# The second layer's modulation as VectorE multiply-adds in the first layer's channel mixing

## The chip, the cores and the metric

One core of a Trainium2 chip. TensorE (PE) multiplies matrices into PSUM, VectorE (DVE) and GpSimd (POOL) work elementwise, ScalarE (ACT) applies functions, SyncE (SP) issues the DMAs. The metric is the device time of one execution in microseconds (us); less is better.

## The reference

A trunk of two layers works on 512 latent tokens and 256 context tokens of 1024 channels, in float32. Each layer scales and shifts its normalized input by a modulation that is worked out from two condition vectors, mixes tokens (convolution and attention), and then mixes channels with a squared-ReLU network of 4096 hidden channels:

```python
mx = (silu_c @ w_ada[i] + b_ada[i])[:, None, :]      # latent: 6 x 1024 values
mc = silu_cc @ w_ada[i] + b_ada[i]                    # context
...
x = x + gx2 * sqrelu_mlp(modulate(rmsnorm(x, norm2_g[i]), sx2, ax2), w_mlp1[i], w_mlp2[i])
if not last:
    h_ctx = h_ctx + gc2 * sqrelu_mlp(modulate(rmsnorm(h_ctx, norm2_g[i]), sc2, ac2),
                                     w_mlp1[i], w_mlp2[i])

def sqrelu_mlp(h, w1, w2):
    return jnp.square(jax.nn.relu(h @ w1)) @ w2
```

The context stream is not needed behind the first layer's end, so the second (`last`) layer's channel mixing has the latent tokens alone.

## The kernel before

**Split products.** Every float32 product is made of three: each operand is split into a rounded high half (`Copy` on ScalarE, L76) and a low half (source minus high half, L77, on VectorE or on the engine in `lo_eng`), and `fm_block` issues high x high, high x low and low x high (L104, L105, L106) for 8 blocks of 128 rows: 24 matmuls for 128 output channels and one group of tokens. A group is the 512 latent tokens (`LAT`, a wide block), the 256 context tokens (`CTXS`, narrow), or around a norm the latent half of 256.

**Weight slabs.** `load_slab` loads 1024 x 256 weights (1 MB) into a raw tile by a DMA on SP's queue and splits them in two halves of four row blocks, `h_w` on ScalarE and `l_w` on `lo_eng`; `both` gives the first half to VectorE and the second to GpSimd. There are two raw tiles (tag `raw`) in this stage, which the modulation's slabs share, and two tiles each for the high and the low halves.

**Channel mixing.** It goes over four chunks of 1024 hidden channels (`cch`). In each, four slabs of `w_mlp1` (tiles `f`; ScalarE relu L1146 into `fr` and square L1147 into the high half `fh`, GpSimd square L1148 of `fr` in place, VectorE subtraction L1149 into the low half `fl`), then four slabs of `w_mlp2` (tiles `r`; VectorE adds the gated product to the residual `X`, L1079). A slab is two blocks of output channels for each group. PSUM tiles: two of tag `mm` for latent blocks, two of tag `mc` for context blocks, four of tag `mi` for the small things. The first chunk starts behind the norm `norm2`, in token groups of 256 and with two slabs held at once; in the last chunk of the first layer `out_slabs` does its last two slabs group by group, with `norm1` of the next layer behind each group (row sums, `dg_n` L253, a matmul that broadcasts them, `nb_n`, then the scaled tokens `nu_n`, split into `h1h` and `h1l`).

**Modulation.** The 6144 modulation columns of a layer are 24 slabs of `w_ada`. `ada_slab` loads one, multiplies it on TensorE by `cvec`, the two condition vectors in 32 columns, into four column strips of the array at once (8 matmuls, L216, two records each), copies the result to SBUF (`adasb`, ScalarE, L222), transposes it (two transposes, L225), adds the four strips up (two reductions, L228) and the bias (L231). The first layer's slabs run before and in its token mixing; the second layer's 24 stand in the first layer's channel mixing, in the loops that the diff shows: one after each slab of weights, two after the first group.

**The order of the work.** The program is written as one order of all engines' work. A scheduler puts it into a fixed queue for each engine before the launch, lets later work go ahead where it is ready by its own plan, and gives out the tiles; on the chip each engine takes its queue in order and waits on semaphores.

Of the kernel before, what the change touches and what calls it, by code (L numbers as in the profile page):

```python
# [8 lines left out]
F32 = mybir.dt.float32  # L9
F32R = mybir.dt.float32r  # L10
AF = mybir.ActivationFunctionType
ALU = mybir.AluOpType
AX = mybir.AxisListType

P = 128
D = 1024
KT = D // P
# [22 lines left out]
R_BADA, R_N1, R_N2, R_BG, R_BDW, R_LNG, R_LNB, R_ANG, R_C, R_CC, R_END = (  # L40
    0, 48, 56, 64, 80, 84, 88, 92, 93, 101, 109)
# [10 lines left out]
def trunk_kernel(  # L52
# [6 lines left out]
    nc = tc.nc  # L59
# [19 lines left out]
    def raw_slab(src, name):  # L79
        r = state["tp"].tile([P, KT, 256], F32, tag="raw", name=name, bufs=state["nraw"])  # L80
        nc.sync.dma_start(r, src)
        return r
# [16 lines left out]
    def rows(src, col0, ncols):  # L99
        return src[:, col0 : col0 + ncols].rearrange("(k p) n -> p k n", p=P)  # L100
# [25 lines left out]
    ident = cst[:, C_ID : C_ID + P]  # L126
# [9 lines left out]
    state = {}  # L136
    both = nc.vector, nc.gpsimd
# [71 lines left out]
    def ada_slab(i, L, s):  # L209

        mi = state["mi"]
        r = raw_slab(rows(w_ada[i], 256 * s, 256), f"ada{i}_{s}")
        ps = mi(f"adaps{i}_{s}")
        for k in range(KT):
            j = k % 4
            nc.tensor.matmul(ps[32 * j : 32 * j + 32, :256], cvec[:, k, :], r[:, k, :],  # L216
                             start=k < 4, stop=k >= 4, tile_position=(0, 32 * j))
        if state["nt"] == 3:
            sb = state["tp"].tile([P, 512], F32, tag="t2k", bufs=3, name=f"adasb{i}_{s}")[:, :256]
        else:  # L220
            sb = spool.tile([P, 512], F32, tag="dg", name=f"adasb{i}_{s}", bufs=1)[:, :256]
        nc.scalar.activation(out=sb, in_=ps[:, :256], func=AF.Copy)  # L222
        pc = ps[:, 256:512]
        for m in range(2):
            nc.tensor.transpose(pc[:, m * P : m * P + P], sb[:, m * P : m * P + P], ident)  # L225
        ad = L["ad"][:, :, 2 * s : 2 * s + 2]
        for q in range(2):
            nc.vector.tensor_reduce(  # L228
                out=ad[:, q], in_=pc.rearrange("p (m j r) -> p m j r", m=2, j=4)[:, :, :, q],
                axis=AX.X, op=ALU.add)  # L230
        nc.vector.tensor_tensor(  # L231
            out=ad, in0=ad,
            in1=L["cols"][:, R_BADA + 2 * s : R_BADA + 2 * s + 2].unsqueeze(1)
            .to_broadcast([P, 2, 2]),
            op=ALU.add)

    def ada_gain(L, which, ks=slice(0, KT)):
        par, r0, nm = ((1, R_N1, "A1"), (4, R_N2, "A2"))[which]
# [71 lines left out]
    for t in range(NTT):  # L310
# [4 lines left out]
        if t == 1:  # L315
            L = layer_params(0)
# [17 lines left out]
    for t in range(NTT):  # L334
        xn = xns[t]
        nc.scalar.activation(out=xn, in_=xrs[t], func=AF.Square, accum_out=rs[:, t : t + 1])
        r = rs[:, t : t + 1]
# [5 lines left out]
    cvec = cpool.tile([P, KT, 32], F32, name="cvec")  # L343
# [3 lines left out]
    for s in range(2):  # L347
        nc.vector.tensor_tensor(
            out=cvec[:, :, s], in0=L["cols"][:, R_C + 8 * s : R_C + 8 * s + 8],
            in1=sg[:, 8 * s : 8 * s + 8], op=ALU.mult)  # L350
# [36 lines left out]
    for i in range(DEPTH):  # L387
        last = i == DEPTH - 1
# [4 lines left out]
        cols = L["cols"]  # L393
# [533 lines left out]
        for half, lst in ((1, ga), (0, gc)):  # L927
            for s in range(4):
# [6 lines left out]
                for m in range(2):  # L935
# [3 lines left out]
                    for g in groups:  # L939
                        W = g.stop - g.start  # L940
# [182 lines left out]

        def mlp1_slab(cch, s):
            w1[cch, s] = load_slab(rows(w_mlp1[i], 1024 * cch + 256 * s, 256),
                                   f"w1_{i}_{cch}_{s}", lo_eng=nc.gpsimd if not last and cch + s < 2 else None)

        out_slabs(lambda s: load_slab(rows(w_out[i], 256 * s, 256), f"wo{i}_{s}"),
                  lambda k: (mh[k], ml[k]), gate1, f"o{i}", norm2, None,
# [9 lines left out]
        for cch in range(4):  # L1139
            fh, fl = [None] * KT, [None] * KT  # L1140
            def hidden(w, mb, m, g):
                W = g.stop - g.start
                ps = ps_for(g, f"f{i}_{cch}_{mb}_{g.start}")
                fm_block(ps[:, :W], w, m * P, lambda k: (h2h[:, k], h2l[:, k]), g)
                r = gp.tile([P, 512], F32, tag="ar", bufs=3, name=f"fr{i}_{cch}_{mb}_{g.start}")
                nc.scalar.activation(out=r[:, :W], in_=ps[:, :W], func=AF.Relu)  # L1146
                nc.scalar.activation(out=fh[mb][:, g], in_=r[:, :W], func=AF.Square)  # L1147
                nc.gpsimd.tensor_tensor(out=r[:, :W], in0=r[:, :W], in1=r[:, :W], op=ALU.mult)  # L1148
                nc.vector.tensor_tensor(out=fl[mb][:, g], in0=r[:, :W], in1=f32(fh[mb][:, g]),  # L1149
                                        op=ALU.subtract)  # L1150

# [3 lines left out]
            for s0 in ((0, 2), (2, 3), (3, 4)) if cch == 0 else ((n, n + 1) for n in range(4)):  # L1155
                for s in range(*s0):
                    if (cch, s) not in w1:
                        mlp1_slab(cch, s)
                ws = {s: w1.pop((cch, s)) for s in range(*s0)}
                for g in halves if cch == 0 and s0[0] == 0 else groups:  # L1160
                    for s in range(*s0):
                        for m in range(2):
                            hidden(ws[s], 2 * s + m, m, g)
                if not last and ada_todo:
                    for _ in range(*s0):
                        ada_slab(i + 1, Ln, ada_todo.pop(0))
            fin = cch == 3
            if fin and not last:
                ada_gain(Ln, 0)
# [17 lines left out]

            def after(s):
                if not last and ada_todo:
                    ada_slab(i + 1, Ln, ada_todo.pop(0))  # L1190
                if fin and not last:
                    nc.sync.dma_start(xs_d[i + 1][:, 2 * s : 2 * s + 2, :],
                                      X[:, 2 * s : 2 * s + 2, :])
                if fin and last:
                    for t in range(4):
                        ps = state["mi"](f"oT{s}_{t}")
                        for m in range(2):
                            nc.tensor.transpose(ps[:, m * P : m * P + P],
                                                X[:, 2 * s + m, t * P : t * P + P], ident)
                        ot = gp.tile([P, 512], F32, tag="t2k", bufs=4, name=f"ot{s}_{t}")  # L1200
                        if t % 2:
                            nc.scalar.activation(out=ot[:, :256], in_=ps[:, :256], func=AF.Copy)
                        else:
                            nc.vector.tensor_copy(ot[:, :256], ps[:, :256])
                        nc.sync.dma_start(out[0, t * P : t * P + P, 256 * s : 256 * s + 256],
                                          ot[:, :256])
# [1 line left out]
            out_slabs(  # L1208
                lambda s: load_slab(
                    w_mlp2[i][1024 * cch : 1024 * cch + 1024, 256 * s : 256 * s + 256]  # L1210
                    .rearrange("(k p) n -> p k n", p=P), f"w2_{i}_{cch}_{s}", lo_eng=None if last else both),
                lambda k: (fh[k], fl[k]), gate2, f"r{i}_{cch}",
                norm1 if fin and not last else None, after,
                (lambda: first.update(w=qk_slab(i + 1, 0, nc.gpsimd)),
                 lambda: first.update(v=v_slab(i + 1, 0, nc.gpsimd))) if fin and not last else ())
        if not last:
            while ada_todo:
                ada_slab(i + 1, Ln, ada_todo.pop(0))
            state["ada_done"] = True
            ada_gain(Ln, 1)  # L1220
            L = Ln
# [77 lines left out]
```

## Time and profile before

| | |
|---|---|
| Median of 3 runs | 2418.24 us (2413.56 to 2418.76) |
| The profiled execution | 2414.77 us, of which the span of its instructions is 2413.0 us |
| TensorE clock granted, mean over the span | 0.985 |
| Busy: TensorE matmuls, VectorE, ScalarE, GpSimd | 2322.9, 1381.9, 933.1, 625.2 us |
| First layer's channel mixing | from 842.8 us to about 1440 us of the span |
| Second layer's channel mixing | from 2046.7 us to the end |

The profile is one execution; times in its views are microseconds from the span's start. A row of a timeline has start, duration, engine, line, operation, the tile written and the tiles read, shapes, and a count where equal instructions are merged; in brackets stand the engine's idle time before it and who ended it. A row of a tile's or line's view has count, then shortest, median and longest duration in nanoseconds. A row of groups has, behind the bar, busy time in us and mean duration in ns, then the idle time before with its releasers. The durations of matmuls are modelled and overlap: the distance from start to start tells their cost. "PEld" is the loading of weights, which runs beside the matmuls.

### The profile page before, as it was taken

Reading aid. Unit: us, or ns where it says so; the run is one execution under the profiler, and the core shown is the slowest. Engines: PE = TensorE matmul, PEld = TensorE weight load, DVE = VectorE, ACT = ScalarE, POOL = GpSimd, SP = SyncE. Lnnn points to the kernel's source line nnn. Section 1 sums busy time; section 2 is a strip of 40 time slices with the busy share of each in tenths; the row PEclk is TensorE's granted clock in tenths of the full one; section 3 lists DMA queues with packets and bytes.
Section 4 is the critical chain, followed back from the end, with each engine's and each line's share of the span. In section 5 each row is a group of like instructions: output and inputs, shape, how many; then the busy total and the mean of one; then the engine's idle time right before and its main releaser. Section 6 shows DMA issues by size and latency. Waiting matters only on the chain.

```text
span 2413.0 us, 36865 instructions
## 1 busy us (share of the span) xinstructions
PE 2322.9 (96%) x15034; PEld 2063.4 (86%) x15034; DVE 1381.9 (57%) x2399; ACT 933.1 (39%) x1839; POOL 625.2 (26%) x786
## 2 busy tenths in 40 slices
PE   7999999999999999999999998999999989999999
PEld 6899998878888988888888998989877869888887
DVE  6877877499766452222222357777749966433333
ACT  5555665522333342221312245555542333422331
POOL 2754655010000131120211255655520000200100
PEclk9999999999999999999999999999999999999999
DMA  8111101144445133333333221111114323232322
GB/s 296 53 38 45 45 27 61 42 135 128 157 148 171 45 103 122 110 119 122 106 122 103 68 75 55 43 40 43 42 59 138 127 70 123 88 105 87 105 87 70
DMA packets 222186, 224.79 MB, mean 93 GB/s; under 512 B 5872, under 2 KB 212160, under 8 KB 221888
## 3 DMA queue, kind: packets, MB, share of 16 engines
q1 hardware_dynamic: 222016, 222.43, 28.6%
q8 instruction: 118, 1.93, 0.3%
q14 instruction: 52, 0.43, 0.1%
HBM read 208.73 MB, written 13.67 MB: 92 GB/s over the span
## 4 chain that ended last, share of the span: by engine, by line
PE 83%; DVE 8%; ACT 3%; POOL 2%; issue 2%; DMA 1%; SPq 0%; ACTq 0%; POOLq 0%; DVEq 0%
PE r L104 6%; PE r L106 6%; PE r L105 6%; PE f L104 6%; PE f L105 6%; PE f L106 6%; PE gt L104 3%; PE gt L106 3%; PE gt L105 3%; PE qk L104 2%; PE qk L105 2%; PE qk L106 2%; PE adaps L216 2%; PE yc L113 2%; PE v L104 2%
## 5 line engine op out<-in xcount | busy, mean ns | idle before, releaser
L104 PE MATMUL r<-fh,h_w 128*128 128x512 f32 (+1 forms) x832 | 285.4, 344 | 0.5 <-DVE X L1079 0.5
L104 PE MATMUL f<-h2h,h_w 128*128 128x512 f32 (+1 forms) x832 | 283.6, 344 | 1.3 <-ACT h2h L76 1.0
L105 PE MATMUL f<-h2l,h_w 128*128 128x512 f32 (+1 forms) x832 | 283.5, 342 | 1.1 <-POOL h2l L77 1.0
L105 PE MATMUL r<-fl,h_w 128*128 128x512 f32 (+1 forms) x832 | 283.2, 341 | 0.0
L106 PE MATMUL r<-fh,l_w 128*128 128x512 f32 (+1 forms) x832 | 283.1, 341 | 0.0
L106 PE MATMUL f<-h2h,l_w 128*128 128x512 f32 (+1 forms) x832 | 281.6, 340 | 0.0
L76 ACT ACTIVATE h_w<-r_w 128x1024 fp32r<-128x1024 f32 x128 | 128.7, 1052 | 313.4 <-PE r L105 131.1
L1148 POOL TENSOR_TENSOR fr<-fr 128x512 f32<-128x512 f32 (+1 forms) x104 | 93.2, 898 | 508.8 <-ACT fh L1147 508.8
L894 DVE SCALAR_TENSOR_TENSOR cacc<-z,cols,cacc 128x783 f32<-128x783 f32 (+1 forms) x240 | 203.3, 900 | 0.4
L104 PE MATMUL qk<-h_wqk,h1h 128*128 128x256 f32 x640 | 185.0, 291 | 4.8 <-ACT h1h L76 3.6
L1079 DVE SCALAR_TENSOR_TENSOR X<-r,ad,X 128x512 f32<-128x512 f32 (+1 forms) x104 | 64.9, 627 | 208.4 <-PE r L106 208.2
L105 PE MATMUL qk<-l_wqk,h1h 128*128 128x256 f32 x640 | 182.2, 286 | 0.0
L106 PE MATMUL qk<-h_wqk,h1l 128*128 128x256 f32 x640 | 178.3, 286 | 0.0
L104 PEld LDWEIGHTS f<-h2h,h_w 128*128 128x128 f32 x832 | 156.6, 189 | 25.1 <-ACT fh L1147 2.5
L104 PEld LDWEIGHTS r<-fh,h_w 128*128 128x128 f32 x832 | 157.6, 190 | 23.8 <-issue 3.7
L105 PEld LDWEIGHTS f<-h2l,h_w 128*128 128x128 f32 x832 | 157.6, 190 | 20.5 <-POOL h2l L77 2.5
L77 DVE TENSOR_TENSOR l_w<-r_w,h_w 128x1024 fp32r<-128x1024 f32 x106 | 126.2, 1222 | 81.8 <-ACT h_w L76 80.2
L106 PEld LDWEIGHTS r<-fh,l_w 128*128 128x128 f32 x832 | 157.7, 190 | 17.7
L106 PEld LDWEIGHTS f<-h2h,l_w 128*128 128x128 f32 x832 | 157.4, 190 | 17.5
L105 PEld LDWEIGHTS r<-fl,h_w 128*128 128x128 f32 x832 | 157.9, 190 | 16.9
L1149 DVE TENSOR_TENSOR fl<-fr,fh 128x512 fp32r<-128x512 f32 (+1 forms) x104 | 62.3, 603 | 189.5 <-POOL fr L1148 189.4
L661 DVE TENSOR_REDUCE st<-S 128x1 f32<-128x768 f32 (+1 forms) x160 | 133.9, 846 | 48.6 <-PE S L659 47.3
(247 smaller groups left out, 6244.8 us busy)
## 6 DMA issues: line engine op xcount, KB each, us to landing
r_w<-in_w_mlp_dram SPq DMA_DIRECT2D x64, 1024.0 KB, 5.5
ada<-in_w_ada_dram SPq DMA_DIRECT2D x48, 1024.0 KB, 5.2
r_wqk<-in_w_in_dram SPq DMA_DIRECT2D x32, 512.0 KB, 5.1
r_wg<-in_w_in_dram SPq DMA_DIRECT2D x16, 1024.0 KB, 5.3
r_wv<-in_w_in_dram SPq DMA_DIRECT2D x8, 1024.0 KB, 5.3
r_wao<-in_w_attn_out_dram SPq DMA_DIRECT2D x8, 1024.0 KB, 5.4
r_wo<-in_w_out_dram SPq DMA_DIRECT2D x8, 1024.0 KB, 7.9
at_d<-uo SPq DMA_DIRECT2D x40, 128.0 KB, 1.7
```

What stands on the lines that cost most here:

```text
L76: nc.scalar.activation(out=hi, in_=src, func=AF.Copy)
L77: (lo_eng or nc.vector).tensor_tensor(out=lo, in0=src, in1=f32(hi), op=ALU.subtract)
L104: nc.tensor.matmul(ps, sh, mh, start=first, stop=False)
L105: nc.tensor.matmul(ps, sh, ml, start=False, stop=False)
L106: nc.tensor.matmul(ps, sl, mh, start=False, stop=last)
L113: nc.tensor.matmul(ps, w[j][:, k, m0 : m0 + P], a(k)[0][:, toks], start=k + j == 0, stop=False)
L216: nc.tensor.matmul(ps[32 * j : 32 * j + 32, :256], cvec[:, k, :], r[:, k, :], start=k < 4, stop=k >= 4, tile_position=(0, 32 * j))
L661: nc.vector.tensor_reduce(out=st[:, m : m + 1], in_=S[:, :nkey], axis=AX.X, op=ALU.max, negate=True)
L894: nc.vector.scalar_tensor_tensor(out=ca[cc][:, :CV], in0=zt[cc][:, t : t + CV], scalar=wcol, in1=ca[cc][:, :CV], op0=ALU.mult, op1=ALU.add)
L1079: nc.vector.scalar_tensor_tensor(out=X[:, mb, g], in0=ps[:, :W], scalar=gate[:, s, mb : mb + 1], in1=X[:, mb, g], op0=ALU.mult, op1=ALU.add)
L1148: nc.gpsimd.tensor_tensor(out=r[:, :W], in0=r[:, :W], in1=r[:, :W], op=ALU.mult)
L1149: nc.vector.tensor_tensor(out=fl[mb][:, g], in0=r[:, :W], in1=f32(fh[mb][:, g]), op=ALU.subtract)
```

## The change

1. The second layer's slabs go through a new `ada_slab_v`: VectorE multiplies the slab's eight row blocks by each condition vector's column and adds them up in a tile of 2 x 256 columns (2 `tensor_scalar` and 14 `scalar_tensor_tensor`), TensorE transposes the four blocks of 128 columns, and VectorE reduces each over its 128 columns and adds the bias. `ada_slab` remains for the first layer's 24.
2. In the first chunk the two slabs after the first group are skipped, so that the modulation begins one group later and ends in the fourth chunk's first half.
3. The square of `fr` in place goes from GpSimd to ScalarE, in both layers.
4. In the first layer all low halves of `w_mlp1` and `w_mlp2` go to GpSimd (before: those of three slabs of `w_mlp1` and the second half of each slab of `w_mlp2`). The second layer's stay on VectorE.

```diff
+    def ada_slab_v(i, L, s):
+        r = raw_slab(rows(w_ada[i], 256 * s, 256), f"ada{i}_{s}")
+        a = state["tp"].tile([P, 512], F32, tag="t2k", bufs=state["nt"], name=f"adaac{i}_{s}")
+        a = a.rearrange("p (q n) -> p q n", q=2)
+        for k in range(KT):
+            for q in range(2):
+                if k == 0:
+                    nc.vector.tensor_scalar(a[:, q], r[:, k], cvec[:, k, q : q + 1], None, ALU.mult)
+                else:
+                    nc.vector.scalar_tensor_tensor(
+                        out=a[:, q], in0=r[:, k], scalar=cvec[:, k, q : q + 1], in1=a[:, q],
+                        op0=ALU.mult, op1=ALU.add)
+        ps = state["mi"](f"adaps{i}_{s}")
+        for n in range(4):
+            nc.tensor.transpose(ps[:, n * P : n * P + P],
+                                a[:, n // 2, n % 2 * P : n % 2 * P + P], ident)
+        ad = L["ad"][:, :, 2 * s : 2 * s + 2]
+        nc.vector.tensor_reduce(out=ad, in_=ps.rearrange("p (q m k) -> p q m k", q=2, m=2),
+                                axis=AX.X, op=ALU.add)
+        nc.vector.tensor_tensor(out=ad, in0=ad, in1=L["cols"][...], op=ALU.add)
...
-    f"w1_{i}_{cch}_{s}", lo_eng=nc.gpsimd if not last and cch + s < 2 else None)
+    f"w1_{i}_{cch}_{s}", lo_eng=None if last else nc.gpsimd)
...
-                nc.gpsimd.tensor_tensor(out=r[:, :W], in0=r[:, :W], in1=r[:, :W], op=ALU.mult)
+                nc.scalar.activation(out=r[:, :W], in_=r[:, :W], func=AF.Square)
...
-                if not last and ada_todo:
+                if not last and ada_todo and cch + s0[0]:
                     for _ in range(*s0):
-                        ada_slab(i + 1, Ln, ada_todo.pop(0))
+                        ada_slab_v(i + 1, Ln, ada_todo.pop(0))
...
             def after(s):
                 if not last and ada_todo:
-                    ada_slab(i + 1, Ln, ada_todo.pop(0))
+                    ada_slab_v(i + 1, Ln, ada_todo.pop(0))
...
-                    ..., f"w2_{i}_{cch}_{s}", lo_eng=None if last else both),
+                    ..., f"w2_{i}_{cch}_{s}", lo_eng=None if last else nc.gpsimd),
```

More of the change, by code (lines that the diff above doesn't have):

```diff
@@ L235, in ada_slab @@
             op=ALU.add)
+    def ada_slab_v(i, L, s):
[17 more added lines that the diff above has]
+                                axis=AX.X, op=ALU.add)
+        nc.vector.tensor_tensor(
+            out=ad, in0=ad,
+            in1=L["cols"][:, R_BADA + 2 * s : R_BADA + 2 * s + 2].unsqueeze(1)
+            .to_broadcast([P, 2, 2]), op=ALU.add)
     def ada_gain(L, which, ks=slice(0, KT)):
@@ L1210, in trunk_kernel @@
                     w_mlp2[i][1024 * cch : 1024 * cch + 1024, 256 * s : 256 * s + 256]
-                    .rearrange("(k p) n -> p k n", p=P), f"w2_{i}_{cch}_{s}", lo_eng=None if last else both),
+                    .rearrange("(k p) n -> p k n", p=P), f"w2_{i}_{cch}_{s}", lo_eng=None if last else nc.gpsimd),
                 lambda k: (fh[k], fl[k]), gate2, f"r{i}_{cch}",
@@ L1217, in trunk_kernel @@
             while ada_todo:
-                ada_slab(i + 1, Ln, ada_todo.pop(0))
+                ada_slab_v(i + 1, Ln, ada_todo.pop(0))
             state["ada_done"] = True
```

## The prediction

> **What bounds the kernel now.** I read the page's totals and slices first, then the busy time of the first layer's channel mixing, then TensorE's timeline around one modulation slab, then the DMA queue.
>
> ```profile
> span 2413.0 us, 36865 instructions
> PE   7999999999999999999999998999999989999999
> DVE  6877877499766452222222357777749966433333
> PE 83%; DVE 8%; ACT 3%; POOL 2%; issue 2%; DMA 1%; SPq 0%; ACTq 0%; POOLq 0%; DVEq 0%
> 870.00:1300.00 430.00, 429.98 (x2714) 364.41 (x2712) 112.93 (x212) 105.44 (x174) 76.86 (x64) 1.00 0.37 118
> ```
>
> The last line is a stretch of the first channel mixing: after its 430.00 us come the busy times of TensorE's matmuls, its weight loads, VectorE, ScalarE and GpSimd. TensorE is busy for 429.98 us and is 83% of the chain that ended last; VectorE has 317 us free. There TensorE's stream of instructions is the time: what leaves it is gained, as long as nobody makes it wait.
>
> **What a slab costs TensorE.** All 24 modulation slabs of the second layer run inside the first layer's channel mixing. One of them in TensorE's timeline (start and duration in us):
>
> ```profile
> 1012.95 0.28 PE L105 MATMUL f<-h2l,h_w 128*128 128x256 f32 x1
> 1013.07 0.28 PE L106 MATMUL f<-h2h,l_w 128*128 128x256 f32 x1
> 1013.27 1.07 PE L216 MATMUL adaps<-ada,cvec 128*32 128x256 f32 x16
> ...
> 1014.61 0.40 PE L105 MATMUL f<-h2l,h_w 128*128 128x512 f32 x1
> 1014.85 0.39 PE L106 MATMUL f<-h2h,l_w 128*128 128x512 f32 x1
> 1015.08 0.40 PE L104 MATMUL f<-h2h,h_w 128*128 128x512 f32 x1
> ...
> 1018.94 0.40 PE L106 MATMUL f<-h2h,l_w 128*128 128x512 f32 x1
> 1019.18 0.38 PE L225 MATMUL adaps<-cst,adasb 128*128 128x128 f32 x2
> ...
> 1019.63 0.39 PE L105 MATMUL f<-h2l,h_w 128*128 128x512 f32 x1
> L216 PE MATMUL adaps<-ada,cvec x384: 379/379/403, 870.1 to 1285.7; 128*32 128x256 f32 x192
> 2382.97 0.44 PE oT L1198 x4
> ```
>
> Durations overlap, so I count start to start. A 256-column matmul takes 0.12 us (1012.95 to 1013.07), a 512-column one 0.23 (1014.85 to 1015.08). From 1013.07 to 1014.61 are 1.54 us for one of each and the slab's matmuls: these cost 1.54 - 0.12 - 0.23 = 1.19. From 1018.94 to 1019.63 are 0.69 us for two 512-column matmuls and the two transposes: 0.69 - 0.46 = 0.23. Together 1.42 us a slab; 384 records at 16 a slab are the 24 slabs.
>
> The new slab needs TensorE for four transposes alone. The last row, from the chain of the last 73 us, is four transposes of the same size between matmuls: 0.44 us. So each slab frees 1.42 - 0.44 = 0.98 us, and **24 x 0.98 = 23.5 us**. Bounds: if two of the four hid completely, 0.23 a slab, 28.6 us; if each group cost twice its 0.44, 13.0 us. I take 0.44, the same operation in the same surroundings.
>
> **VectorE's new work.** Durations are ns, min/median/max or, behind a bar, busy us and mean:
>
> ```profile
> L283 DVE SCALAR_TENSOR_TENSOR h2l<-nu_n,ad,h2h x20: 473/480/951, 830.1 to 2066.2; 128x256 fp32r<-128x256 f32 x20
> L368 DVE TENSOR_SCALAR XN<-XN,A,ad 128x256 f32<-128x256 f32 x8 | 3.2, 407 | 0.0
> L661 DVE TENSOR_REDUCE st<-S 128x1 f32<-128x256 f32 x32 | 13.2, 419 | 15.0 <-PE S L659 14.6
> L661 DVE TENSOR_REDUCE st<-S 128x1 f32<-128x768 f32 x128 | 120.7, 952 | 33.7 <-PE S L659 32.7
> L231 DVE TENSOR_TENSOR ad<-ad,cols x48: 144/163/2366, 24.9 to 1292.3; 128x4 f32<-128x4 f32 x48
> L1079 DVE SCALAR_TENSOR_TENSOR X<-r,ad,X x104: 472/744/753, 931.2 to 2406.7; 128x512 f32<-128x512 f32 x56, 128x256 f32<-128x256 f32 x48
> L77 DVE TENSOR_TENSOR l_w<-r_w,h_w 128x1024 fp32r<-128x1024 f32 x42 | 50.6, 1223 | 30.1 <-ACT h_w L76 30.1
> L77 POOL TENSOR_TENSOR l_w<-r_w,h_w 128x1024 fp32r<-128x1024 f32 x22 | 54.0, 2459 | 185.4 <-ACT h_w L76 185.4
> L76 ACT ACTIVATE h_w<-r_w 128x1024 fp32r<-128x1024 f32 x62 | 62.4, 1053 | 133.7 <-DMA r_w<-in_w_mlp_dram 94.3 <-PE r L105 13.1 <-DVE ad L228 10.2
> ada<-in_w_ada_dram SPq DMA_DIRECT2D x48, 1024.0 KB, 5.2
> ...
> 1068.75 0.37 SPq L90 DMA_DIRECT2D r_w<-in_w_mlp_dram  x1
> 1078.48 0.37 SPq L81 DMA_DIRECT2D ada<-in_w_ada_dram  x1
> 1086.86 0.37 SPq L90 DMA_DIRECT2D r_w<-in_w_mlp_dram  x1
> ```
>
> A slab is 2 tensor_scalar by 0.41, 14 multiply-adds by 0.48, a reduction of 512 elements (between the 0.42 and 0.95 of 256 and 768: 0.69) and an add of 0.16: 0.8 + 6.7 + 0.7 + 0.2 = 8.4 us, 200 us in all. One weight slab now takes 1086.86 - 1068.75 = 18.11 us, afterwards 18.11 - 0.98 = 17.1. In that period VectorE also does four residuals (2 x 0.74 + 2 x 0.47 = 2.4), or about as much subtraction for the hidden layer. 10.8 of 17.1 us: it fits beside TensorE, which is why I cost it at nothing. Without that cover it would cost all of its 200 us.
>
> VectorE works in order, so a residual can stand behind a slab's 16 instructions. Those residuals free the PSUM tiles. A wide block's tile is wanted again after one more wide block (24 matmuls by 0.23 = 5.5 us) and two narrow ones (24 by 0.12 = 2.9 each): 11.3 us later. 8.4 us fits in that; together with a 4.9 us wait for GpSimd (below) it is 13.3 and TensorE would wait 2 us, but only where the whole slab stands in one piece in front of the residual.
>
> **Low halves on GpSimd.** In the first layer 42 half slabs move: VectorE loses 42 x 1.22 = 51 us, GpSimd gains 42 x 2.46 = 103 us and loses the squares of the next fence. A slab's low halves are then ready 1.05 (ScalarE's first half) + 2 x 2.46 = 6.0 us after the previous buffer is released, and usually wanted a period of 17.1 us later: covered by 11 us. Not so where two slabs are held at once (after the first group, and in the last two slabs of the fourth chunk): there the cover is one pair of narrow blocks, 2 x 2.9 = 5.8 us of TensorE, plus half a narrow block (12 by 0.12 = 1.4) until the second half is read: 7.2 against 6.0 just holds; if GpSimd is busy for one more 2.46, it costs 1.3 us at each, 2.6 together.
>
> **The two-input lock.** The row against this change is that VectorE can be held up by GpSimd:
>
> ```profile
> 844.05 4.73 DVE L253 TENSOR_SCALAR dg_n<-cst,ms_n 128x128 f32<-128x128 f32 x2 [0.88 <-POOL ms_n L250]
> 843.98 4.71 POOL L77 TENSOR_TENSOR l_w<-r_w,h_w 128x1024 fp32r<-128x1024 f32 x2
> 848.92 0.67 PE L257 MATMUL nb_n<-dg_n,cst 128*128 128x256 f32 x2 [1.82 <-DVE dg_n L253]
> L253 DVE TENSOR_SCALAR dg_n<-cst,ms_n x16: 276/284/2415, 825.5 to 2057.8; 128x128 f32<-128x128 f32 x16
> ```
>
> Two instructions of 0.28 us ended 4.73 us after the first began, with GpSimd's two low halves (4.71 us), and TensorE waited 1.82. The small add in the fence above shows the same with two inputs from SBUF: 163 ns at the median, 2366 at most. The residual, which has one input in PSUM, never exceeds 753 ns. The new slab's 16 instructions are of the blocked kinds. Priced from these rows, each period's two low halves can hold VectorE up for 4.9 us: 10.8 + 4.9 = 15.7 of 17.1, still under the period. The Trainium skill, SBUF — State Buffer, section Who interferes with whom, states this as a rule: GpSimd and a VectorE instruction in a two-port mode, or with two SBUF inputs, exclude each other for whole instructions. By that rule the trace agrees (4.73 us beside 4.71), and the sum stays where it is as long as the period isn't filled.
>
> **Squares on ScalarE.**
>
> ```profile
> L1147 ACT ACTIVATE fh<-fr 128x512 fp32r<-128x512 f32 x28 | 17.7, 632 | 0.9
> L1148 POOL TENSOR_TENSOR fr<-fr 128x512 f32<-128x512 f32 x28 | 29.8, 1063 | 171.8 <-ACT fh L1147 171.8
> L222 ACT ACTIVATE adasb<-adaps 128x256 f32<-128x256 f32 x24 | 9.2, 382 | 122.5 <-PE adaps L216 120.5 <-PE adaps L225 2.0
> ```
>
> A wide block costs ScalarE 0.63 more in its 5.5 us, and the low half comes 0.4 earlier than with GpSimd's 1.06. ScalarE is busy for 105 of 430 us and loses 24 x 0.38 of copies: no cost, in the second layer too, where TensorE is as full. Beside the first norm its queue is denser; I allow 0 to 1 us.
>
> **The loads.** Modulation and weight slabs share two raw buffers and one SP queue: the weight load at 1068.75 follows a modulation slab's release, the modulation load at 1078.48 a weight slab's. Afterwards a weight slab frees its buffer 6.0 us into a period, the modulation slab lands 5.2 us later and is done 8.4 to 13.3 us after that: 19.6 to 24.5 us into a period that began one slab before the one behind which its transposes stand, so they are due at 2 x 17.1 = 34.2. A cover of 10 us or more. Skipping the first group lets two modulation loads go behind the third weight slab instead of ahead of it: no cost.
>
> **The sum.** The profiled execution took 2414.77 us (span 2413.0 and 1.8 around it), 3.5 under the median of 2418.24. 2414.8 - 23.5 = 2391.3; the small terms (0 to 3.6 us) and the lower bound of 28.6 give the likeliest case a range of 2386 to 2396; the bound of 13.0 alone would give 2402. Forecast **2391**.
>
> **Rivals.** *A, the lock returns part of it.* Near the norms VectorE's sums and small scalings stand behind four more GpSimd halves than now, 2.4 us each, and the two tight places cost 2.6: up to 12 us, 2396 to 2404. For it: the wait of 1.82 us at 848.92. Against: those halves run before the norm begins. The rule of the Trainium skill named above is what A goes by.
>
> *B, slower: TensorE stands at the transposes.* They are in TensorE's queue in a fixed order. If they stand one slab earlier than I think, they are due at 17.1 us and ready at 19.6 to 24.5: a wait of 2.5 to 7.4 us for some 22 slabs, 55 to 163 us, so 2446 to 2554. It decides from 23.5 / 22 = 1.1 us of wait per slab. For it: VectorE's blocked times, which vary from 0.28 to 2.4 us for the same instruction. Against: between 870 and 1300 nothing now makes TensorE wait, and a full TensorE has earlier matmuls to do first.
>
> *C, the gain is eaten.* If VectorE and GpSimd exclude each other more than 4.9 us a period, the loads become the clock at about today's 18.1: 2410 to 2420.
>
> *D, more.* The first slabs now run in pieces and TensorE's waits around the norm may go: 2378 to 2386.
>
> **How the numbers follow.** A measurement here can tell about 0.2%, 5 us. Forecast 0.68, A 0.12, B 0.09, C 0.06, D 0.05. Faster: 0.68 + 0.12 + 0.05 = 0.85; same 0.06; slower 0.09. The range 2383 to 2404 takes in the forecast, A and half of D and leaves out B and C: 0.82.
>
> **What would show it.** Right: 384 fewer L216 records, 96 transposes in their place, weight loads 17.1 us apart, TensorE still full from 870 to 1300, GpSimd with 64 low halves of w, none of them late. Wrong: TensorE idle before the transposes or before r with VectorE as the releaser (B), multiply-adds of 2 us and more with residuals behind them (A, C), or weight loads still 18 us apart (C).

## The result and the profile after

The changed kernel took 2426.86 us (median of four runs, 2424.44 to 2429.7) beside 2415.94 us for the kernel before on the same chip: a ratio of 1.0042, 95% interval 1.0029 to 1.0055. It is slower by 0.4%, where 2391 us, about 1% less than before, was forecast. The profiled execution took 2429.7 us (span 2427.9), 14.9 more than that of before. A fifth run at a granted clock of 0.40 took 7954.52 us, and one of ten runs of the kernel with own buffers below took 4539.38; both are left out of the figures.

Where it lies is found by the first and last matmuls of the first channel mixing (hidden layer f, output r). Before, then after; the columns are duration in ns (min/median/max), first and last start in us, and forms:

```profile
L104 PE MATMUL f<-h2h,h_w x544: 277/283/499, 842.8 to 1352.6; 128*128 128x256 f32 x108, 128*128 128x512 f32 x74
L106 PE MATMUL r<-fh,l_w x576: 279/283/400, 924.3 to 1423.3; 128*128 128x256 f32 x128, 128*128 128x512 f32 x64
```

```profile
L104 PE MATMUL f<-h2h,h_w x544: 277/284/501, 847.8 to 1370.4; 128*128 128x256 f32 x108, 128*128 128x512 f32 x74
L106 PE MATMUL r<-fh,l_w x576: 281/284/629, 926.9 to 1440.6; 128*128 128x256 f32 x128, 128*128 128x512 f32 x64
...
L252 PE MATMUL adaps<-cst,adaac x96: 270/273/328, 876.3 to 1337.3; 128*128 128x128 f32 x96
```

The stage took 1423.3 - 842.8 = 580.5 us before and 1440.6 - 847.8 = 592.8 after. (It also began 5.0 us later; the instructions ahead of it are the same in the same order, and in the twelve other profiles below it began between 842.1 and 848.5, so that part is the execution, not the change.) The 96 transposes are there, and they never waited; what TensorE waited for is other work, in the view of its waits from 760 to 1460 us of the changed kernel (total us, times, longest):

```profile
PE r L105 <- DVE fl L1174: 14.0, 2, 7.6
PE r L104 <- DVE X L1104: 7.6, 3, 3.0
PE f L104 <- DVE X L1104: 5.0, 3, 1.7
```

VectorE is the releaser of each: the hidden layer's subtraction (fl) and the residual (X) came late. With the smaller ones TensorE's waits in the stage are 30.6 us, where they were 1.8 before. VectorE's own waits, 850 to 1370 us, say why:

```profile
DVE adaac L245 <- DMA ada<-in_w_ada_dram: 145.6, 23, 9.0
```

At 23 of the 24 modulation slabs VectorE stood at the first multiplication until the slab had landed, 6.3 us in the mean (145.6 / 23). It works its queue in order, so residuals and subtractions stood behind that wait, whatever share of its time was free.

And the loads were that late because they had become a link in a loop. SyncE's waits show which release a load waited for, first before the change (900 to 1260 us), then after it (925 to 1340 us):

```profile
SPq L90 <- PE adaps L216: 163.0, 20, 12.2
SPq L81 <- DVE l_w L77: 112.6, 19, 8.7
```

```profile
SPq L90 <- DVE adaac L247: 203.6, 20, 11.8
...
SPq L81 <- POOL l_w L77: 5.4, 3, 1.8
```

Weight loads (L90) waited for a modulation slab's release in both kernels; after the change the modulation loads (L81) hardly waited for a buffer of their own, because they stood in SP's queue behind the weight load. One turn of it, from the timelines of SyncE's issues, GpSimd and VectorE (start, duration, instruction; in brackets the idle time before it):

```profile
1050.92 0.37 SPq L90 DMA_DIRECT2D r_w<-in_w_mlp_dram  x1
1051.38 0.53 SPq L81 DMA_DIRECT2D ada<-in_w_ada_dram  x1
1069.51 0.37 SPq L90 DMA_DIRECT2D r_w<-in_w_mlp_dram  x1
1069.97 0.53 SPq L81 DMA_DIRECT2D ada<-in_w_ada_dram  x1
1087.21 0.37 SPq L90 DMA_DIRECT2D r_w<-in_w_mlp_dram  x1
```

```profile
1058.05 4.81 POOL L77 TENSOR_TENSOR l_w<-r_w,h_w 128x1024 fp32r<-128x1024 f32 x2 [13.79 <-ACT h_w L76]
```

```profile
1059.79 3.22 DVE L245 TENSOR_SCALAR adaac<-ada,cvec 128x256 f32<-128x256 f32 x2 [6.88 <-DMA ada<-in_w_ada_dram]
1062.93 3.24 DVE L247 SCALAR_TENSOR_TENSOR adaac<-ada,cvec,adaac 128x256 f32<-128x256 f32 x8
1066.10 0.68 DVE L1174 TENSOR_TENSOR fl<-fr,fh 128x512 fp32r<-128x512 f32 x1
...
1068.22 1.26 DVE L247 SCALAR_TENSOR_TENSOR adaac<-ada,cvec,adaac 128x256 f32<-128x256 f32 x3
```

The weight load of 1069.51 goes out when the last multiply-add of the slab before has ended (1068.22 + 1.26 = 1069.48): it takes that slab's raw buffer. The modulation load follows 0.46 us later into the other buffer, long free. Both megabytes are then on the way together, which the DMA view of 1050 to 1090 us shows (KB each, median us from issue to landing):

```profile
r_w<-in_w_mlp_dram SPq DMA_DIRECT2D x3, 1024.0 KB, 4.9
ada<-in_w_ada_dram SPq DMA_DIRECT2D x3, 1024.0 KB, 8.5
```

The second lands after 8.5 us, where a modulation load took 5.2 before. Meanwhile the weights have landed, ScalarE has rounded its first half, and GpSimd's two low halves run from 1058.05 to 1062.86. The two multiplications, 0.62 us for a pair that nothing holds (one at 792.43 in the kernel with own buffers below), are held until 1063.01. Then come the fourteen multiply-adds with the subtractions between them, and the buffer is free again. The turn is 1069.51 - 1050.92 = 18.6 us: 0.5 until the modulation load's issue, 8.4 until VectorE can start and 9.7 until its last multiply-add ends. The next is 17.7; from the weight load at 938.35 to that at 1292.60 the 19 turns took 18.6 in the mean. TensorE wanted 17.1, the distance of the weight loads where nothing holds them (below).

The last part is the clock. The windows view (PE, PEld, DVE, ACT and POOL busy us with instruction counts, the granted clock, DMA share, GB/s) of 10 us around the end of the longest wait and of the 10 us after them, and from TensorE's timeline the first matmul behind the wait and the first one at the usual distance again:

```profile
1080.60:1090.60 10.00, 6.08 (x14) 4.79 (x15) 8.34 (x21) 0.00 (x0) 0.00 (x0) 0.50 0.24 76
1090.80:1100.80 10.00, 10.00 (x70) 9.30 (x69) 5.70 (x15) 1.45 (x2) 0.31 (x1) 1.00 0.39 126
```

```profile
1084.53 0.80 PE L105 MATMUL r<-fl,h_w 128*128 128x512 f32 x1 [7.63 <-DVE fl L1174]
...
1090.94 0.39 PE L105 MATMUL r<-fl,h_w 128*128 128x512 f32 x1
```

The granted clock was 0.50 in the first 10 us and 1.00 in the next. The wait ended at 1084.53, but the 15 matmuls from there to 1090.94 took 6.4 us, where 15 at the usual 0.23 take 3.5: the wait cost 3.0 us more than its length. Behind the wait of 6.4 us, which ended at 1234.88, 14 matmuls took 6.1 us instead of 3.2. The stage thus adds up: 580.5, less 24.6 (what TensorE saves, measured below with next to no waits), plus 28.8 more of waits is 584.7. Of the 8.1 missing to 592.8 these two stretches are 5.9. The granted clock was 0.50 in two shorter stretches as well (855.3 to 858.5 and 879.2 to 882.4 us); that they are the rest is likely, but not shown.

### The profile page after: what moved, and what is told of

Its sections match the earlier page's. It is cut to its first block, busy times and chain, and to the rows that moved or that the text cites. A ratio compares the mean times of both kernels' runs of the same rounds, so it can differ in the third digit from the quotient of the medians.

```text
span 2427.9 us, 36376 instructions
## 1 busy us (share of the span) xinstructions
PE 2303.0 (95%) x14698; PEld 2062.0 (85%) x14698; DVE 1551.3 (64%) x2717; ACT 978.8 (40%) x1919; POOL 642.5 (26%) x724
## 4 chain that ended last, share of the span: by engine, by line
PE 67%; DVE 17%; DMA 8%; POOL 3%; ACT 3%; issue 2%; SPq 0%; ACTq 0%; POOLq 0%; DVEq 0%
DMA ada<-in_w_ada_dram 6%; DVE adaac L247 5%; PE r L105 4%; PE r L106 4%; PE r L104 4%; PE f L105 4%; PE f L104 4%; PE f L106 4%; PE gt L104 3%; PE gt L105 3%; PE gt L106 3%; PE qk L104 3%; PE qk L105 3%; PE qk L106 3%; DVE adaac L245 2%
## 5 line engine op out<-in xcount | busy, mean ns | idle before, releaser
L77 POOL TENSOR_TENSOR l_w<-r_w,h_w 128x1024 fp32r<-128x1024 f32 x64 | 160.4, 2526 | 377.2 <-ACT h_w L76 377.2
L105 PEld LDWEIGHTS r<-fl,h_w 128*128 128x128 f32 x832 | 159.4, 192 | 32.7 <-DVE fl L1174 14.9
L247 DVE SCALAR_TENSOR_TENSOR adaac<-ada,cvec,adaac 128x256 f32<-128x256 f32 x336 | 158.2, 528 | 0.0
L245 DVE TENSOR_SCALAR adaac<-ada,cvec 128x256 f32<-128x256 f32 x48 | 60.5, 1300 | 145.6 <-DMA ada<-in_w_ada_dram 145.6
L689 ACT ACTIVATE e<-S,st 128x768 f32<-128x768 f32 (+1 forms) x160 | 130.3, 817 | 48.0 <-DVE st L686 45.0
```

What stands on the lines that cost most here:

```text
L77: (lo_eng or nc.vector).tensor_tensor(out=lo, in0=src, in1=f32(hi), op=ALU.subtract)
L105: nc.tensor.matmul(ps, sh, ml, start=False, stop=False)
L245: nc.vector.tensor_scalar(a[:, q], r[:, k], cvec[:, k, q : q + 1], None, ALU.mult)
L247: nc.vector.scalar_tensor_tensor(out=a[:, q], in0=r[:, k], scalar=cvec[:, k, q : q + 1], in1=a[:, q], op0=ALU.mult, op1=ALU.add)
L689: nc.scalar.activation(out=e[:, :nkey], in_=S[:, :nkey], func=AF.Exp, bias=st[:, m : m + 1], accum_out=st[:, 2 + m : 3 + m])
```

## The experiments

Times are medians beside the kernel before on the same chip (2415.1 to 2415.8 us in the four groups). Theory 1 is the loop just told. Its rivals: the lock of GpSimd alone, the waiting of VectorE's queue at loads alone, one of the other edits.

**Modulation back on TensorE, the rest of the change kept.**

```diff
-                    ada_slab_v(i + 1, Ln, ada_todo.pop(0))
+                    ada_slab(i + 1, Ln, ada_todo.pop(0))
```

> The changed kernel with the second layer's modulation back on TensorE (the old slab function, still begun behind the norm); squares on ScalarE and low halves on GpSimd stay. Theory 1 (the load loop: a weight load and the next modulation load leave SP's queue together, only when the last slab's multiply-adds have released their raw tile; they land 8.7 us later and the multiply-adds take 8.4 + 2.6 us, more than the 17.1 us period): the loop is gone, so about the kernel before, 2413 to 2419 us. Theory 2 (GpSimd's low halves lock VectorE out): VectorE has little to do here, 2413 to 2419 too. Rival R (the squares or the later low halves cost by themselves): 2420 to 2428.

2413.4 us, ratio 0.9998 (0.9982 to 1.0014): squares on ScalarE, low halves on GpSimd and the later start cost nothing by themselves.

**A raw buffer for each kind of load** (one and one, in place of two for both).

```diff
-        r = state["tp"].tile([P, KT, 256], F32, tag="raw", name=name, bufs=state["nraw"])
+        own = state["nt"] == 4
+        r = state["tp"].tile([P, KT, 256], F32, tag="rawa" if own else "raw", name=name,
+                             bufs=1 if own else state["nraw"])
...
-        state["tp"], state["nraw"], state["nt"] = gp, 2, 4
+        state["tp"], state["nraw"], state["nt"] = gp, 2 if last else 1, 4
```

> The changed kernel with the two raw tiles of the first layer's channel mixing given one to the weights and one to the modulation, so that neither waits for the other's release; nothing else changed. Theory 1 (load loop): the weight load no longer waits for the multiply-adds and no longer shares the DMA engines with the modulation load; loop 5.2 + 8.4 + up to 2.6 = 14 to 16 us, under 17.1: TensorE's waits on VectorE fall from 26 us to under 6, 2393 to 2402 us. Theory 2 (lock): GpSimd's work is the same, 2415 to 2428. Theory 3 (VectorE's queue: whatever the loop, residuals stand behind an instruction that waits for a load): the wait shrinks from 8.7 to 5.2 us, about half the loss is left, 2405 to 2412.

2405.61 us, ratio 0.9965 (0.9951 to 0.998): 21 us faster than the changed kernel, and short of the 2393 to 2402 expected. TensorE's waits from 840 to 1410 us:

```profile
PE f L107 <- DVE h2l L310: 3.5, 2, 3.0
PE f L107 <- POOL h2l L77: 2.2, 2, 1.9
```

No wait for fl or X is left; these lie at the first norm, and are dealt with below.

**Low halves on VectorE** (nearly all; three of the early slabs stay on GpSimd).

```diff
-                                   f"w1_{i}_{cch}_{s}", lo_eng=None if last else nc.gpsimd)
+                                   f"w1_{i}_{cch}_{s}", lo_eng=nc.gpsimd if not last and cch + s < 2 else None)
...
-                    .rearrange("(k p) n -> p k n", p=P), f"w2_{i}_{cch}_{s}", lo_eng=None if last else nc.gpsimd),
+                    .rearrange("(k p) n -> p k n", p=P), f"w2_{i}_{cch}_{s}", lo_eng=None),
```

> The changed kernel with all low halves of the channel mixing's weights on VectorE, so that GpSimd has no work there and cannot lock VectorE out. Theory 1 (load loop): the multiply-adds lose their 2.6 us of blocking, VectorE gains 2.4 us of low halves, the loop is 8.7 + 8.4 + 0 to 2.4 = 17.1 to 19.5 us: little changes, 2412 to 2426 us, VectorE still waits 7 to 9 us per slab for the load. Theory 2 (lock): the loss is gone, 2390 to 2398.

2404.98 us, ratio 0.9954 (0.994 to 0.9968), between the two expectations. The multiplications fell from a mean of 1300 ns to 357, though VectorE had 1.2 us more to do per half slab; TensorE's waits in the stage fell to 11.6 us. The loop was still there: from the weight load at 942.36 to that at 1283.03 the 19 turns took 17.9 us in the mean, less than 18.6 but over 17.1. So the lock was worth about as much as the buffer, which theory 1 had put too low.

**A quarter of the multiply-adds.** Two of the eight row blocks are multiplied; the other six are left out. The loads stay whole.

```diff
-        for k in range(KT):
+        for k in (0, KT - 1):
```

> The changed kernel with only the first and the last of the eight row blocks of each of the second layer's modulation slabs multiplied and added (4 of 16 VectorE instructions; the whole slab is still loaded); the other six are left out. Theory 1 (load loop): 8.7 + 3.2 + 2.6 = 14.5 us, under 17.1, the waits go, 2390 to 2398 us. Theory 2 (lock): the first instructions are blocked as before, but the slab is short: 2395 to 2405. Theory 3 (residuals behind an instruction that waits for a load): the wait for the load stays, 2408 to 2420.

2389.69 us, ratio 0.9901 (0.988 to 0.9922). VectorE's waits for the slabs (850 to 1370 us) and TensorE's stage:

```profile
DVE adaac L245 <- DMA ada<-in_w_ada_dram: 86.2, 24, 6.0
```

```profile
L104 PE MATMUL f<-h2h,h_w x544: 277/283/477, 843.7 to 1326.7; 128*128 128x256 f32 x108, 128*128 128x512 f32 x74
L106 PE MATMUL r<-fh,l_w x576: 281/283/398, 918.0 to 1396.9; 128*128 128x256 f32 x128, 128*128 128x512 f32 x64
```

VectorE still stood at all 24 loads, 3.6 us each, yet TensorE waited only 2.3 us in the stage, and the weight loads from 946.85 to 1254.68 came 17.1 us apart (18 turns): waiting at a load was harmless here, where the loop closed in time. This also prices TensorE's saving with next to no waits on either side: the stage was 577.8 us with the modulation back on TensorE and is 1396.9 - 843.7 = 553.2 here, 24.6 us less.

**Half of each modulation load.** Four row blocks are loaded and used twice; the other four are left out.

```diff
-        nc.sync.dma_start(r, src)
+        nc.sync.dma_start(r[:, :nk], src[:, :nk])
...
-        r = raw_slab(rows(w_ada[i], 256 * s, 256), f"ada{i}_{s}")
+        r = raw_slab(rows(w_ada[i], 256 * s, 256), f"ada{i}_{s}", KT // 2)
...
-                        out=a[:, q], in0=r[:, k], scalar=cvec[:, k, q : q + 1], in1=a[:, q],
+                        out=a[:, q], in0=r[:, k % 4], scalar=cvec[:, k, q : q + 1], in1=a[:, q],
```

> The changed kernel, but each modulation load fetches only four of its eight row blocks (0.5 MB instead of 1 MB) and the sixteen vector instructions read those four twice; what is left out: the other half of the modulation's weights. Theory 1 (a serial loop: paired loads, then the lock of the two GpSimd low halves, then the multiply-adds): the weight load has less beside it, so it lands a little earlier (about 4 instead of 5 us after its issue), but the low halves that follow it still run until some 10 to 11 us after the issue and hold the two first multiplies; the loop gets 0.5 to 1 us shorter of 17.9 and the time falls to 2408-2420 us. Rival (the arrival of the modulation slab, 8.7 us after the issue, is what the loop waits for, the lock adds little behind it): it lands at 6 to 7, the loop drops below 17.1, TensorE's waits fall under 12 us and the time is 2395-2406.

2409.79 us, ratio 0.9963 (0.9947 to 0.9978). As long as the two loads went out together, until 1080 us, the slab landed 6.0 to 6.7 us after its issue, and the groups of the stage (count, busy us, mean ns) show where the lock went:

```profile
L247 DVE SCALAR_TENSOR_TENSOR adaac<-ada,cvec,adaac 128x256 f32<-128x256 f32 x336 | 169.1, 567 | 0.0
L257 DVE TENSOR_TENSOR ad<-ad,cols 128x4 f32<-128x4 f32 x24 | 33.2, 1382 | 0.8
L245 DVE TENSOR_SCALAR adaac<-ada,cvec 128x256 f32<-128x256 f32 x48 | 28.5, 636 | 81.9 <-DMA ada<-in_w_ada_dram 81.9
```

The multiplications are held less (636 ns instead of 1300), but the multiply-adds behind them more (567 instead of 528), and so are the small bias additions (1382 instead of 527): VectorE meets GpSimd's halves some instructions later. Turns stayed at 17.5 to 18.3 us until 1080 us, so the loop got shorter by a part of what the load did.

**The modulation on VectorE alone**, low halves and squares as before the change (the second matrices' halves one on each engine).

```diff
-                                   f"w1_{i}_{cch}_{s}", lo_eng=None if last else nc.gpsimd)
+                                   f"w1_{i}_{cch}_{s}", lo_eng=nc.gpsimd if not last and cch + s < 2 else None)
...
-                    .rearrange("(k p) n -> p k n", p=P), f"w2_{i}_{cch}_{s}", lo_eng=None if last else nc.gpsimd),
+                    .rearrange("(k p) n -> p k n", p=P), f"w2_{i}_{cch}_{s}", lo_eng=None if last else both),
...
-                nc.scalar.activation(out=r[:, :W], in_=r[:, :W], func=AF.Square)
+                nc.gpsimd.tensor_tensor(out=r[:, :W], in0=r[:, :W], in1=r[:, :W], op=ALU.mult)
```

> The modulation on VectorE alone: low halves as before the change (first weight matrices of a chunk on VectorE, the second ones one half on each engine) and squares on GpSimd as before. Theory 1: the lock is shorter (one GpSimd half or none instead of two), VectorE has 1.2 to 2.4 us a period more of its own; the loop stays near 17.1 to 18 and the time is 2403-2418 us, near that of the kernel with all low halves on VectorE (2405). Rival (the squares on GpSimd, two of about 1 us per block, lock VectorE as much as the low halves did): 2418-2430.

2405.27 us, ratio 0.9957 (0.9945 to 0.997). So the move of the modulation gains 10 us, the other edits nothing alone, and all together lose about 11: with the experiment on the low halves, it is these on GpSimd, put into the turn of a loop that the modulation had closed, that cost.

**Own buffers, every modulation load held behind its step's weight load, start one step later.** The edit for own buffers is the one above.

```diff
+        with tc.issue_after(state["load"].ins):
+            r = raw_slab(rows(w_ada[i], 256 * s, 256), f"ada{i}_{s}")
...
-                if not last and ada_todo and cch + s0[0]:
+                if not last and ada_todo and cch + s0[0] > 2:
```

> Each kind of load has a raw tile of its own (one and one, the same memory as the two shared ones), each modulation load is issued behind the weight load of its step, and the first slab is begun one step later. Theory 1: with its own tile the modulation no longer closes the loop, and with the load held back none of its multiply-adds falls into the norm, where the kernel with own tiles lost 9.6 us of TensorE; the time is 2391-2399 us, TensorE's waits in the first channel mixing under 4 us. Rival (the 12 us that the own tiles were short of the forecast lie in the lock or in the rest of the program): 2402-2408.

2408.2 us, ratio 0.996 (0.9944 to 0.9976): a miss, and the rival's number. SyncE's issues:

```profile
996.91 0.37 SPq L92 DMA_DIRECT2D r_w<-in_w_mlp_dram  x1
997.37 0.53 SPq L83 DMA_DIRECT2D ada<-in_w_ada_dram  x1
```

The hold paired several of the loads again (0.46 us apart), VectorE stood 107.3 us at them, and fl was late once (3.6 us). And the first norm's waits stayed (3.1 for h2l, 1.2 for h2h), although no multiply-add ran there any more: my reason for them was wrong.

**The same, low halves shared as before the change.**

> As the kernel before it in this list, with the low halves shared between VectorE and GpSimd as before the change. Theory 1: once the loop is open, the lock costs TensorE nothing, so this one is within 4 us of the other, 2389-2400 us. Rival (the lock still costs TensorE directly): 5 to 10 us faster than the other one.

2414.27 us, ratio 0.9987 (0.9975 to 0.9999): 6 us slower than the one above, outside both expectations. TensorE waited 9.3 us for fl. SyncE's largest wait (1010 to 1360 us):

```profile
SPq L92 <- DVE l_w L77: 180.8, 12, 17.0
```

In the kernel above the weight loads waited for GpSimd's low halves. Here they waited for VectorE's, and these stood in its queue among the multiply-adds of a slab whose load had been held behind the same weight load: the low half that began at 1189.46 ended at 1190.67, and the weight load followed at 1190.74. So the hold has closed a new loop. From 1154.63 to 1320.56 the 9 turns took 18.4 us in the mean, where the kernel above had 17.0 in the same stretch.

**Own buffers, and at the norms both for the weights.** What was left to explain the norm's waits was that the weights had lost their second buffer there. Here they use the modulation's where none runs; only the first modulation load is held.

```diff
+        alt = state["nt"] == 4 and name in ("wo0_3", "w1_0_0_1", "w2_0_3_3", "wv1_0")
+        r = state["tp"].tile([P, *shape], F32, tag="rawa" if alt else "raw", name=f"r_{name}",
+                             bufs=1 if alt else state["nraw"])
...
+        with tc.issue_after(state["load"].ins) if s == 0 else contextlib.nullcontext():
```

> Own raw tiles as in the second kernel, with two edits: where no modulation slab is under way (the two norms at either end of the first channel mixing), the weights use the modulation's tile as a second one, and the first modulation load is held behind the load of the third weight slab, so that none is begun inside the norm. Theory (own tiles open the loop; what they lost again, 9.6 us of TensorE's waits at the first norm and about 6 us behind the last one, came from weights that had only one tile there, so that their splits fell among ScalarE's norm instructions, and from the half clock after each such wait): TensorE's waits in the first channel mixing fall to 2-5 us, its length to 552-558 us, the stage after it goes back to 622-626, and the time is 2386-2396 us. Rival (the waits at the norms come from the modulation itself or from the lock): waits stay at 8-10 us and the time at 2402-2408.

2398.37 us, ratio 0.9934 (0.9921 to 0.9948): 17 us faster than before, 28 faster than the changed kernel, though 2 us above the range expected. The issues, the waits at buffers on SyncE (900 to 1370 us) and the windows:

```profile
1048.08 0.37 SPq L95 DMA_DIRECT2D r_w<-in_w_mlp_dram  x1
1054.18 0.37 SPq L84 DMA_DIRECT2D ada<-in_w_ada_dram  x1
1065.18 0.37 SPq L95 DMA_DIRECT2D r_w<-in_w_mlp_dram  x1
...
1082.28 0.37 SPq L95 DMA_DIRECT2D r_w<-in_w_mlp_dram  x1
```

```profile
SPq L95 <- POOL l_w L78: 260.3, 26, 12.0
SPq L84 <- DVE adaac L253: 112.8, 19, 6.8
```

```profile
843.00:1000.00 157.00, 150.92 (x935) 136.18 (x934) 121.64 (x238) 54.77 (x108) 55.82 (x28) 0.98 0.39 125
1000.00:1200.00 200.00, 200.00 (x1179) 178.11 (x1178) 154.37 (x257) 70.64 (x117) 55.77 (x24) 1.00 0.39 124
1200.00:1400.00 200.00, 200.00 (x1341) 185.41 (x1340) 88.78 (x149) 59.26 (x102) 56.98 (x27) 1.00 0.26 86
```

Weight loads wait for low halves and modulation loads for multiply-adds, each kind for its own; they are 6 us apart, the weight loads come every 17.1 us, TensorE is full from 1000 to 1400 at a clock of 1.00. The stage takes 560.0 us, 20.5 of the 24.6 less; it has 6.1 us of waits, all at the first norm, and the clock of 0.98 around them, which is where the rest most likely went.

**With that, the low halves on VectorE, and the low halves and squares as before.**

> As the kernel before it in this list, with all low halves of the first layer's channel mixing on VectorE (1.21 us each, two a slab). Theory: with the loop open the lock costs TensorE nothing, so this kernel is not faster; VectorE's load per period rises by 2.4 us to about 13.5 of 17.1, and the time is within 5 us of the other, on the slow side if anything (2388-2400). Rival (the lock still costs TensorE a part): 4 to 10 us faster than the other one.

> As the first of this list, with the low halves and the squares where they were before the change (so only the modulation is moved). Theory: squares and low halves carry nothing of the gain once the loop is open, so the time is within 5 us of the other two, 2386-2400. Rival (the three edits belong together: without the squares on ScalarE and the low halves on GpSimd VectorE is too full): TensorE's waits rise by 5 us or more and the time is 2398-2410.

2397.14 us (ratio 0.993, 0.9918 to 0.9942) and 2398.4 us (0.9939, 0.9926 to 0.9951): within 1.3 us of each other and of the kernel above. The 2398.4 lies in the theory's range and in the rival's, but TensorE's waits decide for the theory: 6.3 us in the stage beside 6.1 in the kernel above. In that kernel the lock is longer than in the changed one (its multiplications took 1951 ns in the mean, there 1300). Here one pair from its VectorE timeline:

```profile
1060.32 4.98 DVE L251 TENSOR_SCALAR adaac<-ada,cvec 128x256 f32<-128x256 f32 x2
```

4.98 us for two multiplications, and it costs nothing that the times show: the weight load no longer waits for what comes behind them.

**The control: the kernel before, with the same handling of the buffers.**

> The kernel before the change, modulation on TensorE, with the two raw tiles handled as in the fastest kernel (one for weights, one for the modulation's slabs and, at the norms, a second one for weights; first modulation load held back). Theory: before the change nothing waited at these tiles (TensorE waited 1.8 us in the first channel mixing), so the handling of the tiles is worth nothing by itself: 2410-2421 us, ratio 0.998 to 1.002. Rival (the own tiles are the gain, and moving the modulation adds little): 2398-2408.

2415.9 us, ratio 1.0 (0.999 to 1.001). The buffers alone give nothing; the 17 us are the modulation's move, once its loop is open.

## Why the prediction was wrong

**TensorE's work: right.** 23.5 us were forecast, 24.6 measured between the two kernels with next to no waits. The kernel with a quarter of the multiply-adds took 2389.7; the forecast was 2391.

**VectorE's work: right in sum.** 8.4 us a slab was forecast; the multiply-adds took 528 ns in the changed kernel and 489 with little lock, against 480, and the busy time fitted the period. But "it fits beside TensorE" was a statement on busy time, and the engine works in order: it stood idle 6.3 us a slab at a load with TensorE's residuals behind it. The prediction weighed such a queue only for the 16 instructions and the lock, 13.3 us against a cover of 11.3, and let that pass as a rare 2 us. The wait at the load comes on top, and made the two waits of 6.4 and 7.6 us.

**The loads: the step that failed.** The prediction said that a weight slab frees its buffer 6.0 us into a period, that the modulation slab lands 5.2 later, is done 19.6 to 24.5 us into the period and is due at 34.2. For the transposes that cover held: they never waited. What failed is the order of the buffers under it, which the prediction took over from the kernel before and gave no reason for. It said that a weight load follows a modulation slab's release, and did not ask which slab's. Before the change it was the last but one: the weight load of 1068.75 waited for the matmuls on the twelfth of the 24 modulation slabs (1067.61 + 1.07 = 1068.68), loaded at 1041.57, while the thirteenth, loaded at 1060.36, lay in the other buffer. In that order a buffer has two periods for its round. In the changed kernel, from 938 us on, each weight load took the buffer of the last modulation slab, and the next modulation load stood behind it in the queue. That round has to close in one period. In the prediction's own terms it takes 5.2 us for the load and 8.4 to 13.3 for the work, 13.6 to 18.5 in all, whose upper end was over the 17.1 that TensorE wanted. The runs showed 18.6, with two terms different: the loads went out together, so the second took 8.5 instead of 5.2, and the lock took 2.6 of the 4.9 (3.22 - 0.62).

The switch is in the trace: four issues, and what SyncE waited for at the first three of them.

```profile
915.40 0.37 SPq L90 DMA_DIRECT2D r_w<-in_w_mlp_dram  x1
921.43 0.37 SPq L81 DMA_DIRECT2D ada<-in_w_ada_dram  x1
938.35 0.37 SPq L90 DMA_DIRECT2D r_w<-in_w_mlp_dram  x1
938.80 0.53 SPq L81 DMA_DIRECT2D ada<-in_w_ada_dram  x1
```

```profile
SPq L90 <- POOL l_w L77: 8.6, 1, 8.6
SPq L81 <- DVE adaac L247: 5.6, 1, 5.6
SPq L90 <- DVE adaac L247: 11.8, 1, 11.8
```

At 915.40 and 921.43 each load took the buffer of its own kind, as in the experiments with own buffers; at 938.35 the weight load took the modulation's. TensorE's first wait for the residual ended at 969 us, 31 us behind the switch. Why the program hands the buffers out in the other order from there on stays open.

**The lock: right in size, wrong in place.** "15.7 of 17.1, still under the period" added the lock to busy time. It belongs in the loop, where there was no room; with the loop open the same lock is free (2398.4 with 4.98 us of it, 2397.1 with almost none).

**Low halves and squares: right alone.** Their cost is nothing without the modulation on VectorE (2413.4) and nothing with own buffers (2398.4). In the closed loop GpSimd's halves cost 22 us (2426.9 beside 2405.0 with them on VectorE).

**The clock: not in the sum.** I priced a wait of TensorE at its length; 28.8 us of waits cost 36.9. The Trainium skill (TensorE: Matmul & The Clock Gate, Part 1) says that the clock falls to half after an idle window of about 3.4 us and returns after a busy one. By that rule the trace agrees in kind: half clock for about 10 us around a wait of 7.6. In the small it does not: the granted clock was also 0.50 behind waits of 1.8 and 1.7 us (855.3 and 879.2), and it stayed at 1.00 around waits of 3.0 and 2.9 (966 to 976 and 986 to 996 us). No run here changed the clock without the waits.

**The rivals.** C came nearest: weight loads about 18 us apart, as its sign said. Its condition did not hold, the exclusion was under 4.9 us; and its 2410 to 2420 was low: the loads came every 18.6 us, not every 18.1, which is 10 us over the 19 turns. B named the right direction and the wrong place. Of the signs that the prediction named for being wrong, TensorE's transposes did not wait, but TensorE was idle before r with VectorE as the releaser, and multiplications and multiply-adds were held for 2 us and more with residuals behind them.

## What to carry to other kernels

When work moves to an engine with time to spare, follow its buffers all the way round: load, wait, work, release, next load. Add that loop up against the period, not busy time against the period, and add every lock and every shared transfer in it. Ask of each load not only that a buffer is released for it, but which one. Two kinds of load that share buffers can tie their consumers together; one buffer for each, in the same memory, opened this loop, and with both of them for the weights at the norms it turned 0.4% slower into 0.7% faster.

## What the hardware showed that I had not expected

- Two 1 MB loads issued 0.46 us apart land after 4.9 and 8.5 us; one alone took 5.2. The first one loses nothing; the second lands 3.3 us later than alone.
- A TensorE wait costs more than itself when the clock falls: behind a wait of 7.6 us the granted clock stayed at 0.50 for 6 us, and the matmuls in them took 3.0 us more than usual.
- GpSimd's hold on VectorE shifted rather than vanished: with the modulation slab landing about 2 us earlier, the 48 multiplications went from 1300 to 636 ns, 32 us less in all, and the 336 multiply-adds from 528 to 567 and the 24 bias additions from 527 to 1382, 34 us more.
